# Ending each block of neighbourhood attention by itself, at four places of a head pair

## The chip, the cores and the metric

The kernel runs on one core of one Trainium2 chip. The core has a matrix engine (PE: matmuls, with PEld for its weight loads), a vector engine (DVE), a scalar engine for activation functions (ACT), a general engine (POOL), a queue engine (SP) that issues transfers, and 16 DMA engines. Each engine works through its own queue in order and waits at an instruction until what it needs is there. The metric is the time of one execution on the device in microseconds (us); it was run three times, and the median counts.

## The reference, cut to what matters

Two layers are computed on 2048 latent tokens (a grid of 32 rows by 64 columns) and 256 context tokens, of width 1024. The change is in the attention of layer 1 alone. There, each of 16 heads (64 wide) lets every token look at a window of 8 x 16 tokens around it and at all context tokens:

```python
def one_row(args):
    qr, r = args
    ...
    s_lat = jnp.einsum('bqhd,brkhd->bhqrk', qr, kb, preferred_element_type=jnp.float32) * scale
    s_lat = s_lat + bias.astype(jnp.float32)[None]
    s_lat = jnp.where(col_mask[None, None, :, None, :], s_lat, -jnp.inf).reshape(...)
    s_ctx = jnp.einsum('bqhd,bchd->bhqc', qr, k_ctx, preferred_element_type=jnp.float32) * scale
    p = jax.nn.softmax(jnp.concatenate([s_lat, s_ctx], axis=-1), axis=-1).astype(v.dtype)
    o = jnp.einsum('bhqk,bkhd->bqhd', p[..., :kr * GRID_W], vb.reshape(bsz, kr * GRID_W, h, d))
    return o + jnp.einsum('bhqc,bchd->bqhd', p[..., kr * GRID_W:], v_ctx)
...
y = jnp.dot(o.reshape(h.shape[0], h.shape[1], C_WIDTH) * jax.nn.silu(z_x), w_out)
```

## The kernel before, in words

Layer 1's attention is the function `odd_attention`. Everything stays in float32 accuracy: q and k are each split into a high and a low part.

**Pairs, tiles, blocks.** The 16 heads are taken as 8 pairs (`j` from 0 to 7), one head on the lower 64 partitions and one on the upper 64. The 2048 queries of a pair form four blocks of 512 (8 grid rows each). The keys are cut the other way: 16 latent key tiles (`n` from 0 to 15: four groups of 8 grid rows by four groups of 16 columns) and two context key tiles. A latent key tile is looked at by a rectangle of queries that reaches over two or three blocks; a context tile is looked at by all, block after block. This makes 24 score tiles a pair: 16 latent and 4 x 2 context ones, in the order `units`: context tiles of block 0, latent tile 0, context of block 1, latent tiles 1 to 3, context of block 2, latent 4 to 7, context of block 3, latent 8 to 15. Block 0 has all its parts after latent tile 7, block 1 after tile 11, blocks 2 and 3 after tile 15.

**One score tile.** PE writes the scores (`scores`, L1785: eight matmuls) into a buffer `st` of PSUM. There are only two of these (two banks each), so the scores of a tile wait until those of the tile before last have been read. For a latent tile DVE reads them: it adds the bias table (L1961) and writes to a buffer `opt` in SBUF, of which there are 11; ACT then takes the exponential in place (L108, a helper of all activations). For a context tile ACT reads the scores itself. Some tiles later the tile's tail follows: PE multiplies the exponentials with the values and accumulates into one PSUM bank `o` for each block, of which there are four (L1797 for context, L1815 for latent tiles), and POOL adds the exponentials to `oacc`, the sums for the denominators (L1821; one buffer for blocks 0 and 1, one for 2 and 3). Tails are collected in the list `pend` and put out two at a time by `flush`, whenever five are pending. The sums of two context tiles start `oacc` (L1806, on DVE for the even blocks, on POOL for the odd ones).

**Ending blocks.** `finish_blocks` ends one or two blocks: PE sums `oacc` over the partitions, times -2 (L1840, the denominators, into an `st` buffer); ACT copies them to SBUF, takes the logarithm and then the exponential of its negative, which is the reciprocal; DVE multiplies denominator and reciprocal (L1849, for a correction step), the reciprocal and the gates (L1851), corrects the accumulated output (L1854), multiplies it with the gated reciprocal (L1855); POOL issues the store to `RT1` (L1856). The function is a generator in three parts: denominators and copy; the logarithm; all the rest. `flush` starts it (list `late`: after how many flushes, which blocks), and `end` puts out one part after each score tile. Before the change, pairs 0 to 6 end blocks 0 and 1 together after tile 11's tail and blocks 2 and 3 together after tile 15's tail. Tails lag behind the scores, so both endings fall into the beginning of the next pair. The last pair ends block 0 after tile 7, block 1 after tile 11, and 2 and 3 together.

**Gates and order.** The gates of a pair (`z1`, two halves of 1024 queries) are loaded by `gates` into one buffer, `os4`, on SP's queue. All these loads are in one chain. A call `issue_after(x)` places the instructions issued under it behind the instruction `x` in the scheduler's order; otherwise the order of the code decides. So an engine's queue mixes biases, exponentials, tails and endings, and what stands ahead in a queue is done first.

After pair 7's tiles comes the output projection. During pair 7 its weights are loaded into `opt` buffers and split into high and low parts on ACT and DVE (L1299).

Of the kernel before, what the change touches and what calls it, by code (L numbers as in the profile page):

```python
# [17 lines left out]
P = 128  # L18
D = 1024
# [69 lines left out]
class Kern:  # L89
# [1630 lines left out]
    def odd_attention(self, out, pools, left, wout):  # L1720
# [4 lines left out]
        with ExitStack() as es:  # L1725
# [82 lines left out]
            def tail(n, pts, j, V, O, acc, _):  # L1808
                g, c = divmod(n, 4)
                (r0, nr), (c0, w) = rect("k", g, c)  # L1810
                done = {7: [0], 11: [1], 15: [2, 3]}.get(n, [])
# [10 lines left out]
                if n == 11:  # L1822
                    done = [1] if j == 7 else [0, 1]
                elif j < 7 and n == 7:
                    done = []
                if done:
                    late.append([2 if (j, n) == (7, 15) else 1, done, j, O, acc])
                return mm

            def gates(j, hf):  # L1830
                Z[j, hf] = self.tl(gp, [P, D], "os4", bufs=1)
                self.load(Z[j, hf][:], self.z1[j, :, hf * D : hf * D + D])

            def finish_blocks(bbs, j, O, acc):

                n, hf, o0 = len(bbs), bbs[0] // 2, bbs[0] % 2 * 512
# [11 lines left out]
                self.act(rc[:, :n], ln[:, :n], AF.Exp, scale=-1.0)  # L1848
                nc.vector.tensor_tensor(out=ln[:, :n], in0=dc[:, :n], in1=rc[:, :n], op=ALU.mult)  # L1849
                flat = rc[:, :n].rearrange("p b c -> p (b c)")  # L1850
                nc.vector.tensor_tensor(out=flat, in0=flat, in1=Z[j, hf][:, o0 : o0 + n * 512], op=ALU.mult)  # L1851
                for b, bb in enumerate(bbs):
                    o = O.pop(bb)[:].rearrange("p r c -> p (r c)")
                    nc.vector.scalar_tensor_tensor(out=o, in0=ln[:, b], scalar=2.0, in1=o, op0=ALU.add, op1=ALU.mult)  # L1854
                    nc.vector.tensor_tensor(out=rc[:, b], in0=o, in1=rc[:, b], op=ALU.mult)  # L1855
# [31 lines left out]
            Q, K, V, Z, tabs, raw = {}, {}, {}, {}, {}, {}  # L1887
# [11 lines left out]
            pend, late, ends, OA, first_sums = [], [], [], {}, {}  # L1899
# [20 lines left out]
            def end(after):  # L1920

                with self.tc.issue_after(after.ins):
                    if ends and next(ends[0], self) is self:
                        ends.pop(0)

            for j in range(8):
                OA[j] = {}, {}
                for s, (kind, n, u) in enumerate(units):
                    g, c = divmod(n, 4)
                    if s in (1, 10) and j + s > 1:  # L1930
                        gates(*((j - 1, 1) if s == 1 else (j, 0)))
# [38 lines left out]
                    end(ex)  # L1970
# [61 lines left out]
            while ends:  # L2032
                end(ex)
# [3 lines left out]
            while ends:  # L2037
                end(ex)
# [185 lines left out]
```

## Time and profile before

| what | us |
|---|---|
| median of three runs | 3561.03 |
| lowest and highest of the three | 3557.43, 3561.45 |
| the profiled execution | 3562.45 |
| its span in the profile | 3560.7 |
| PE busy in the span | 3446.4 (97%) |
| DVE, ACT, POOL busy | 2411.3, 1463.3, 1041.8 |
| mean granted clock of PE | 0.987 |

The span runs from the first instruction to the last; the execution's own time is 1.75 us longer. Layer 1's attention lies between about 2960 and 3400 us of the span. A timeline row reads: start, length, engine, line, operation, output and inputs by the program's names, shape, count, and in brackets how long the engine was idle before and what ended that. Rows of instructions that overlap or follow closely are merged. The chain of waits is followed back from the last instruction. PEq, SPq and the like are an engine's queue.

### The profile page before, as it was taken

The page shows a single profiled execution, that of the slowest core. Times are in us where ns is not written, and L with a number is a line of the kernel's source. Part 1 is how long each engine was busy: PE and PEld are TensorE (multiplying, and loading weights), DVE is VectorE, ACT ScalarE, POOL GpSimd, SP SyncE. Part 2 cuts the span into 40 slices and gives each one's busy share as a digit, 9 for nine tenths or more (in the row PEclk, how much of TensorE's full clock was granted, in tenths as well). Part 3 has the DMA queues.
Part 4 walks back from the last instruction along what each step waited for, and adds up shares of the span by engine and source line. Part 5 has one row for each costly group of instructions (what it writes and reads, how often), then busy time and mean ns, then how long its engine had stood idle before and what let it go on. Part 6 is the DMA issues. An engine that isn't in the chain of part 4 may idle for free.

```text
span 3560.7 us, 54719 instructions
## 1 busy us (share of the span) xinstructions
PE 3446.4 (97%) x20228; PEld 2671.1 (75%) x20228; DVE 2411.3 (68%) x4494; ACT 1463.3 (41%) x2570; POOL 1041.8 (29%) x1281
## 2 busy tenths in 40 slices
PE   7999998999999999999999999999999999888899
PEld 6898997888886666665557878888888886555577
DVE  4677665888885777768876654555578883555765
ACT  5454552111114554546663344454322224555532
POOL 1333431111111333322211133333111115766611
PEclk9999999999999999999999999999999999999999
DMA  7555555233315242434526764445745546454374
GB/s 255 148 155 163 146 147 157 86 98 95 105 64 162 72 132 74 124 101 145 157 82 153 149 187 150 156 129 178 226 151 171 156 121 221 160 199 176 110 186 63
DMA packets 349888, 508.40 MB, mean 143 GB/s; under 512 B 32443, under 2 KB 232843, under 8 KB 342661
## 3 DMA queue, kind: packets, MB, share of 16 engines
q1 hardware_dynamic: 297364, 386.91, 35.8%
q0 software_dynamic: 29232, 82.14, 8.7%
q10 hardware_dynamic: 23024, 35.85, 2.9%
q8 instruction: 160, 2.62, 0.3%
q14 instruction: 108, 0.88, 0.1%
HBM read 325.99 MB, written 196.60 MB: 147 GB/s over the span
## 4 chain that ended last, share of the span: by engine, by line
PE 80%; DVE 7%; DMA 5%; ACT 3%; issue 2%; POOL 2%; SPq 1%; DVEq 0%; ACTq 0%; POOLq 0%
PE gm L133 10%; PE gm L131 10%; PE gm L132 10%; PE st L1175 10%; PE av L1085 7%; PE mx L705 4%; PE st L1785 4%; PE o L1815 2%; PE o L1364 2%; PE pu L1364 2%; PE st L1364 1%; PE pj L1364 1%; PE mx L1697 1%; ACT opt L108 1%; DMA adaw<-ada_w 1%
## 5 line engine op out<-in xcount | busy, mean ns | idle before, releaser
L706 DVE TENSOR_REDUCE mm<-mx 128x1 f32<-128x512 f32 (+1 forms) x656 | 389.4, 629 | 85.1 <-PE mx L705 78.1
L108 ACT ACTIVATE apt<-st 128x1024 f32<-128x1024 f32 (+1 forms) x296 | 300.2, 1015 | 303.7 <-PE st L1175 284.4
L1182 DVE TENSOR_TENSOR acc<-acc,apt 128x1024 f32<-128x1024 f32 x256 | 340.7, 1331 | 83.2 <-ACT apt L108 64.3
L1175 PE MATMUL st<-aq,akh 64*128 64x512 f32 x1728 | 312.2, 408 | 1.3 <-ACT apt L108 1.0
L1085 PE MATMUL av<-apt,av 128*64 128x512 f32 x1152 | 265.8, 598 | 0.0
L1821 POOL TENSOR_TENSOR oacc<-oacc,opt 128x528 f32<-128x528 f32 (+4 forms) x192 | 227.6, 1207 | 73.8 <-ACT opt L108 67.6
L705 PE MATMUL mx<-mk,mq 96*128 96x512 f32 (+1 forms) x656 | 236.1, 373 | 5.3 <-DMA mq<-QC 5.3
L1175 PE MATMUL st<-aq,akl 64*128 64x512 f32 (+1 forms) x1152 | 230.7, 390 | 0.0
L1961 DVE TENSOR_TENSOR opt<-st,tab 128x496 f32<-128x496 f32 (+16 forms) x288 | 124.5, 485 | 148.4 <-PE st L1785 148.4
L108 ACT ACTIVATE u<-gm 128x352 f32<-128x352 f32 (+1 forms) x140 | 68.7, 497 | 375.7 <-PE gm L133 206.2
L1703 DVE CUSTOM_DVE_ANT_1 mx<-mx,mtab 128x105 f32<-128x105 f32 (+14 forms) x576 | 183.0, 340 | 49.3 <-PE mx L1697 35.4
L1175 PEld LDWEIGHTS st<-aq,akh 64*128 64x128 f32 x1728 | 152.9, 185 | 82.8 <-ACT apt L108 29.4
L1085 PEld LDWEIGHTS av<-apt,av 128*64 128x64 f32 x1152 | 76.3, 136 | 135.2 <-issue 133.9
L108 ACT ACTIVATE opt<-opt 128x930 f32<-128x930 f32 (+9 forms) x130 | 104.9, 807 | 147.7 <-DVE opt L1961 140.1
L1785 PE MATMUL st<-qh,kh 64*128 64x512 f32 (+6 forms) x384 | 84.2, 432 | 53.0 <-DVE opt L1961 47.2
L705 PEld LDWEIGHTS mx<-mk,mq 96*128 96x128 f32 x656 | 121.7, 189 | 17.1 <-issue 5.7
L1175 PEld LDWEIGHTS st<-aq,akl 64*128 64x128 f32 (+1 forms) x1152 | 112.3, 184 | 22.8
L1785 PEld LDWEIGHTS st<-qh,kh 64*128 64x128 f32 x384 | 38.0, 190 | 110.9 <-issue 73.4
L220 POOL TENSOR_TENSOR oss<-oss,mhalf 128x8 f32<-128x8 f32 x68 | 112.3, 1651 | 5.4
L131 PE MATMUL gm<-w1h,hhi 128*128 128x512 f32 x280 | 111.9, 400 | 0.1
L1552 DVE TENSOR_TENSOR onat<-gm,oss 128x512 f32<-128x512 f32 x68 | 46.9, 690 | 95.6 <-POOL oss L220 95.6
L131 PE MATMUL gm<-w0h,hhi 128*128 128x512 f32 x272 | 110.1, 405 | 0.0
(777 smaller groups left out, 9692.1 us busy)
## 6 DMA issues: line engine op xcount, KB each, us to landing
H<-x ACTq DMA_DIRECT2D x32, 512.0 KB
adaw<-ada_w SPq DMA_DIRECT2D x64, 256.0 KB
wraw<-w_od SPq DMA_DIRECT2D x64, 256.0 KB
K1t<-okt POOLq DMA_DIRECT2D x16, 1024.0 KB, 6.6
x<-H SPq DMA_DIRECT2D x31, 512.0 KB
mtab<-rpb_q SPq DMA_DIRECT2D x16, 899.0 KB
x<-xin SPq DMA_DIRECT2D x18, 512.0 KB
x<-xin POOLq DMA_DIRECT2D x18, 512.0 KB, 5.3
```

The source lines that it names most:

```text
L108: return self.nc.scalar.activation(out, in_, func, **kw)
L131: self.nc.tensor.matmul(out, lh(k), rh(k), start=start and j == 0, stop=False)
L132: self.nc.tensor.matmul(out, lh(k), rl(k), start=False, stop=False)
L133: yield self.nc.tensor.matmul(out, ll(k), rh(k), start=False, stop=stop and j == n - 1)
L705: mm = nc.tensor.matmul(ps[:, :w], q[:A_QK, (t % 6) * P : (t % 6) * P + P], k[:A_QK, k0 : k0 + w], start=True, stop=True)
L706: nc.vector.tensor_reduce(out=m[:, t, n : n + 1], in_=ps[:, :w], axis=AX.X, op=ALU.max)
L1085: mm = nc.tensor.matmul(O[j, nb][i * 64 : i * 64 + 64, :w], V[j, kt // TT][:, kt % TT, i * 64 : i * 64 + 64], pts[:, i, :w], start=n == 0, ...
L1175: mm = nc.tensor.matmul(ps[:, o // 64, :w], k[o : o + r, kb, kq], Q[o : o + r, qb, :w], start=m == 0, stop=m == 4)
L1182: added = nc.vector.tensor_tensor(out=acc[:, :, :w], in0=a[:, :, :w], in1=pts[:, :, :w], op=ALU.add)
L1364: self.mm = self.nc.tensor.matmul(ps, x[:, k, :], y, start=start and k == 0 and n == 0, stop=k == self.H4 - 1 and n == 2, skip_group_check ...
L1785: mm = nc.tensor.matmul(ps(i), ones[s] if k is None else k[s, ks], qs(q[s]), start=n == 0, stop=n == 3)
L1821: nc.gpsimd.tensor_tensor(out=a, in0=a, in1=pts[:, :, a0 - r0 : a1 - r0, :], op=ALU.add)
```

## The change

`tail` now hands every block to `late` by itself: block 0 after tile 7's tail and block 1 after tile 11's, in the next flush; block 2 three flushes after tile 15's tail and block 3 five flushes after it. The last pair still ends its blocks 2 and 3 together, as before. `finish_blocks` has five parts in place of three: denominators and copy; logarithm; reciprocal; the two multiplications; the rest and the store. A block 0 is put out at once, as the last pair's was before. `end` places a part behind both the tile's last bias and its exponential, where it was behind the exponential alone. The gates of the second half get a buffer of their own, `ogate` (the output projection uses it later), except in the last pair, and their load is placed two score tiles later.

```diff
                     nc.gpsimd.tensor_tensor(out=a, in0=a, in1=pts[:, :, a0 - r0 : a1 - r0, :], op=ALU.add)
-                if n == 11:
-                    done = [1] if j == 7 else [0, 1]
-                elif j < 7 and n == 7:
-                    done = []
-                if done:
-                    late.append([2 if (j, n) == (7, 15) else 1, done, j, O, acc])
+                if (j, n) == (7, 15):
+                    late.append([2, done, j, O, acc])
+                else:
+                    late.extend([{2: 3, 3: 5}.get(bb, 1), [bb], j, O, acc] for bb in done)
                 return mm
 
             def gates(j, hf):
-                Z[j, hf] = self.tl(gp, [P, D], "os4", bufs=1)
+                Z[j, hf] = self.tl(gp, [P, D], "ogate" if hf and j < 7 else "os4", bufs=1)
...
                 self.act(rc[:, :n], ln[:, :n], AF.Exp, scale=-1.0)
+                yield
                 nc.vector.tensor_tensor(out=ln[:, :n], in0=dc[:, :n], in1=rc[:, :n], op=ALU.mult)
                 flat = rc[:, :n].rearrange("p b c -> p (b c)")
                 nc.vector.tensor_tensor(out=flat, in0=flat, in1=Z[j, hf][:, o0 : o0 + n * 512], op=ALU.mult)
+                yield
                 for b, bb in enumerate(bbs):
...
-            def end(after):
-
-                with self.tc.issue_after(after.ins):
-                    if ends and next(ends[0], self) is self:
+            def end():
+
+                if not ends:
+                    return
+                with self.tc.issue_after(ex.ins), self.tc.issue_after(bias.ins):
+                    if next(ends[0], self) is self:
                         ends.pop(0)
...
-                    if s in (1, 10) and j + s > 1:
-                        gates(*((j - 1, 1) if s == 1 else (j, 0)))
+                    if s in (3, 10) and j + s > 3:
+                        gates(*((j - 1, 1) if s == 3 else (j, 0)))
...
-                    end(ex)
+                    end()
```

What this does to the queues is shown at three places. Line numbers behind the change are higher by two for the biases (L1963) and lower by one or two at the top of the ending (L1838 for the denominators, L1848 and L1850 for the first two multiplications); L1854 and L1855 are the same.

DVE at the start of a middle pair (`rl` and `opt` with 1024 or 512 elements: endings; `opt<-st,tab`: biases), before:

```order
L1849 TENSOR_TENSOR rl_28924<-opt_28907,opt_28937 128x1024
L1851 TENSOR_TENSOR opt_28937<-opt_28937,os_4956_28650 128x1024
L1854 SCALAR_TENSOR_TENSOR o_28561<-rl_28924,o_28561 128x512
L1854 SCALAR_TENSOR_TENSOR o_28598<-rl_28924,o_28598 128x512
L1961 TENSOR_TENSOR opt_28970<-st_28969,tab_28566 128x2x4x8
L1961 TENSOR_TENSOR opt_28970<-st_28969,tab_28566 128x2x4x16
L1961 TENSOR_TENSOR opt_28970<-st_28969,tab_28566 128x2x8x8
L1961 TENSOR_TENSOR opt_28970<-st_28969,tab_28566 128x2x8x16
L1806 TENSOR_TENSOR oacc_4999_28984<-opt_28927,opt_28959 128x2x512
L1855 TENSOR_TENSOR opt_28937<-o_28561,opt_28937 128x512
L1855 TENSOR_TENSOR opt_28937<-o_28598,opt_28937 128x512
L1849 TENSOR_TENSOR rl_29020<-opt_29001,opt_29037 128x1024
```

The same place now:

```order
L1848 TENSOR_TENSOR rl_28956<-opt_28939,opt_28969 128x512
L1850 TENSOR_TENSOR opt_28969<-opt_28969,os_4960_28653 128x512
L1963 TENSOR_TENSOR opt_28995<-st_28994,tab_28558 128x2x4x8
L1963 TENSOR_TENSOR opt_28995<-st_28994,tab_28558 128x2x4x16
L1963 TENSOR_TENSOR opt_28995<-st_28994,tab_28558 128x2x8x8
L1963 TENSOR_TENSOR opt_28995<-st_28994,tab_28558 128x2x8x16
L1806 TENSOR_TENSOR oacc_5010_29009<-opt_28959,opt_28982 128x2x512
L1854 SCALAR_TENSOR_TENSOR o_28590<-rl_28956,o_28590 128x512
L1855 TENSOR_TENSOR opt_28969<-o_28590,opt_28969 128x512
L1963 TENSOR_TENSOR opt_29066<-st_29065,tab_28558 128x2x124
L1963 TENSOR_TENSOR opt_29066<-st_29065,tab_28558 128x2x248
```

Only block 1's ending, at half the width, is left around latent tile 0's four biases; the biases of tile 1 follow it, where the first multiplication of blocks 2 and 3 stood.

DVE around latent tiles 9 to 11 of the same pair, before:

```order
L1961 TENSOR_TENSOR opt_29273<-st_29272,tab_28566 128x2x465
L1961 TENSOR_TENSOR opt_29285<-st_29284,tab_28566 128x2x465
L1961 TENSOR_TENSOR opt_29302<-st_29301,tab_28566 128x2x15x16
L1961 TENSOR_TENSOR opt_29302<-st_29301,tab_28566 128x2x15x7
L1961 TENSOR_TENSOR opt_29315<-st_29314,tab_28566 128x2x8x8
```

Now:

```order
L1963 TENSOR_TENSOR opt_29327<-st_29326,tab_28558 128x2x465
L1848 TENSOR_TENSOR rl_29317<-opt_29315,opt_29319 128x512
L1963 TENSOR_TENSOR opt_29339<-st_29338,tab_28558 128x2x465
L1850 TENSOR_TENSOR opt_29319<-opt_29319,os_5038_29158 128x512
L1854 SCALAR_TENSOR_TENSOR o_29058<-rl_29317,o_29058 128x512
L1855 TENSOR_TENSOR opt_29319<-o_29058,opt_29319 128x512
L1963 TENSOR_TENSOR opt_29356<-st_29355,tab_28558 128x2x15x16
L1963 TENSOR_TENSOR opt_29356<-st_29355,tab_28558 128x2x15x7
```

Block 0's ending has come between the biases of tiles 9, 10 and 11, where there were biases alone.

POOL at latent tiles 8 to 11 of the same pair (sums; the last name is the tile's exponentials), before:

```order
L1821 TENSOR_TENSOR oacc_4999_28984<-oacc_4999_28984,opt_29285 128x2x3x31
L1821 TENSOR_TENSOR oacc_5031_29172<-oacc_5031_29172,opt_29285 128x2x12x31
L1821 TENSOR_TENSOR oacc_4999_28984<-oacc_4999_28984,opt_29302 128x2x3x23
L1821 TENSOR_TENSOR oacc_5031_29172<-oacc_5031_29172,opt_29302 128x2x12x23
L1821 TENSOR_TENSOR oacc_5031_29172<-oacc_5031_29172,opt_29315 128x2x11x24
```

Now:

```order
L1821 TENSOR_TENSOR oacc_5010_29009<-oacc_5010_29009,opt_29339 128x2x3x31
L1821 TENSOR_TENSOR oacc_5045_29203<-oacc_5045_29203,opt_29339 128x2x12x31
L1856 DMA RT<-opt_29319 128x512
L1821 TENSOR_TENSOR oacc_5010_29009<-oacc_5010_29009,opt_29356 128x2x3x23
L1821 TENSOR_TENSOR oacc_5045_29203<-oacc_5045_29203,opt_29356 128x2x12x23
```

Block 0's store now stands between the sums of tile 10 and those of tile 11.

More of the change, by code (lines that the diff above doesn't have):

```diff
@@ L2032, in odd_attention @@
             while ends:
-                end(ex)
+                end()
             gates(7, 1)
@@ L2037, in odd_attention @@
             while ends:
-                end(ex)
+                end()
             PLAIN, h4 = 4, self.H4
```

## The prediction

> **What bounds the kernel now.** I read the windows from one denominator of blocks 0 and 1 to the next first, then the chain, then PE's and DVE's timelines of one pair. Chain (start, length, engine and line):
>
> ```profile
> 3005.99 1.72 PE st L1840 x8
> ...
> 3317.87 1.72 PE st L1840 x8
> ```
>
> Seven of these denominators, six periods between them: (3317.87 - 3005.99) / 6 = 51.98 us. Windows (us, PE busy, PEld, DVE, ACT, POOL, granted clock, DMA share, GB/s) of one period, of a piece inside it, and of the last pair:
>
> ```profile
> 3110.29:3161.95 51.66, 45.32 (x402) 28.47 (x400) 28.65 (x50) 26.43 (x31) 34.07 (x29) 0.97 0.47 172
> ...
> 3134.00:3136.00 2.00, 1.60 (x8) 0.96 (x9) 2.00 (x6) 0.83 (x1) 0.68 (x1) 0.73 1.01 425
> 3136.00:3138.00 2.00, 2.00 (x15) 1.48 (x16) 0.28 (x2) 1.57 (x2) 1.60 (x3) 0.50 0.98 401
> 3138.00:3140.00 2.00, 2.00 (x22) 1.46 (x18) 0.00 (x0) 0.36 (x1) 1.09 (x1) 0.91 1.11 338
> ...
> 3317.87:3384.20 66.33, 50.93 (x406) 31.02 (x404) 52.85 (x70) 37.18 (x51) 38.54 (x30) 0.90 0.37 121
> ```
>
> In a period no engine but PE is near full, and PE idles 6.3 us of it. PE's timeline shows where (in brackets the idle time before, and what ended it):
>
> ```profile
> 3110.12 1.89 PE L1840 MATMUL st<-oacc,mtwos 128*64 128x512 f32 x8
> ...
> 3113.21 0.50 PE L1785 MATMUL st<-qh,kh 64*128 64x512 f32 x2 [0.52 <-ACT opt L108]
> ...
> 3118.38 1.94 PE L1840 MATMUL st<-oacc,mtwos 128*64 128x512 f32 x8
> 3122.10 0.50 PE L1785 MATMUL st<-qh,kh 64*128 64x512 f32 x2 [1.78 <-DVE opt L1961]
> ...
> 3130.86 0.41 PE L1785 MATMUL st<-qh,kh 64*128 64x288 f32 x2 [1.29 <-DVE opt L1961]
> ...
> 3134.40 0.50 PE L1785 MATMUL st<-qh,kh 64*128 64x512 f32 x2 [2.74 <-DVE opt L1961]
> ```
>
> 0.52 + 1.78 + 1.29 + 2.74 = 6.33 us, all in the first 25 us; from there to the next denominator PE has no gap. The clock rows add a second loss: after the idle stretch the granted clock is 0.73, 0.50 and 0.91 in three windows of 2 us, 0.54 + 1.00 + 0.18 = 1.7 us. So PE's own work is 51.66 - 6.33 - 1.72 = 43.6 us. DVE's timeline over the same stretch names the cause:
>
> ```profile
> 3112.85 0.90 DVE L1961 TENSOR_TENSOR opt<-st,tab 128x272 f32<-128x272 f32 x4 [2.84 <-PE st L1785]
> 3117.35 1.23 DVE L1849 TENSOR_TENSOR rl<-opt,opt 128x1024 f32<-128x1024 f32 x1 [3.60 <-ACT opt L108]
> 3118.67 1.23 DVE L1851 TENSOR_TENSOR opt<-opt,os 128x1024 f32<-128x1024 f32 x1
> 3119.81 1.29 DVE L1854 SCALAR_TENSOR_TENSOR o<-rl,o 128x512 f32<-128x512 f32 x2
> 3121.01 0.94 DVE L1961 TENSOR_TENSOR opt<-st,tab 128x64 f32<-128x64 f32 x4
> ...
> 3127.25 2.56 DVE L1849 TENSOR_TENSOR rl<-opt,opt 128x1024 f32<-128x1024 f32 x1 [2.97 <-ACT opt L108]
> 3129.73 0.98 DVE L1961 TENSOR_TENSOR opt<-st,tab 128x248 f32<-128x248 f32 x2
> 3130.64 1.51 DVE L1851 TENSOR_TENSOR opt<-opt,os 128x1024 f32<-128x1024 f32 x1
> ```
>
> The endings of two block pairs follow each other. Bias additions (L1961), which alone free the two score buffers, stand in DVE's queue behind 1024-wide multiplications that wait for ACT: 3.60 and 2.97 us of waiting with biases queued behind it.
>
> **The change, part by part.** What one block's ending costs can be read in the last pair, which already ends blocks 0 and 1 singly (ACT, then DVE):
>
> ```profile
> 3366.70 0.58 ACT L108 ACTIVATE opt<-st 128x512 f32<-128x512 f32 x1
> 3367.30 0.63 ACT L108 ACTIVATE rl<-opt 128x512 f32<-128x512 f32 x1
> ...
> 3369.93 1.32 DVE L1849 TENSOR_TENSOR rl<-opt,opt 128x512 f32<-128x512 f32 x1
> ...
> 3372.21 1.63 DVE L1851 TENSOR_TENSOR opt<-opt,os 128x512 f32<-128x512 f32 x1
> 3373.76 0.68 DVE L1854 SCALAR_TENSOR_TENSOR o<-rl,o 128x512 f32<-128x512 f32 x1
> ...
> 3376.30 0.68 DVE L1855 TENSOR_TENSOR opt<-o,opt 128x512 f32<-128x512 f32 x1
> ...
> 3391.09 0.76 DVE L1849 TENSOR_TENSOR rl<-opt,opt 128x512 f32<-128x512 f32 x1 [1.84 <-ACT opt L108]
> ```
>
> The last row's time is the first multiplication with POOL idle, 1.32 and 1.63 are both with POOL at work. The same shows at full width: 1.23 us at 3117.35 and 2.56 at 3127.25, where POOL's timeline has
>
> ```profile
> 3102.41 13.64 POOL L1821 TENSOR_TENSOR oacc<-oacc,opt 128x144 f32<-128x144 f32 x12
> 3124.81 0.55 POOL L1856 DMA_DIRECT2D RT<-opt  x1 [8.76 <-ACT opt L108]
> 3126.35 2.38 POOL L1806 TENSOR_TENSOR oacc<-opt,opt 128x1024 f32<-128x1024 f32 x1 [0.99 <-ACT opt L108]
> 3128.80 2.27 POOL L1821 TENSOR_TENSOR oacc<-oacc,opt 128x576 f32<-128x576 f32 x1
> ```
>
> Counts for a pair: PE keeps its 16 denominator matmuls, in four groups of 0.9 us in place of two of 1.72, so its 43.6 us stay. ACT gets six instructions more, each half as long: 4 x (0.58 + 0.63 + 0.63) against 2 x 3.1 is +1.2 us, hidden in the 25 us in which ACT idles; what counts is where PE waits for a copy. DVE has the same elements. Now the waits that are left, from the start of block 1's denominator (time 0):
>
> (a) The copy of the denominator holds a score buffer. Before, the next scores waited 0.52; the denominator and copy are now 0.86 and 0.44 shorter, of which the scores of tile 15, in between, take part: 0.1, and as much after block 2's: 0.2.
>
> (b) Block 1's first multiplication ran at 3117.35, 7.06 after 3110.29. The denominator takes 0.86 less and Ln and Exp 0.4 less each: 5.4. Behind it stand the second one and tile 0's bias, 0.76 + 0.7 + 0.94 without POOL, 1.32 + 1.63 + 0.94 with it: the buffer is free at 7.8 to 9.3. PE comes to that buffer after 3118.38 - 3110.12 - 1.72 - 0.52 = 6.0 us of work, the short denominator (0.9), the wait (0.1) and one tile's scores (1.0, half of the two tiles' 1.98 in the chain below): 8.0. A wait of 0 to 1.3; 0.5, POOL being nearly through its run of sums. The waits of 1.29 and 2.74 go: nothing but biases is left in DVE's queue there.
>
> (c) Block 2's two multiplications go ahead of tile 4's bias, block 3's four operations ahead of tile 8's. PE has attention-value products and a denominator to do there (over 2 us before it needs the buffer). Bounds 0 and 0.9, and 0 and 0.6: I take 0.5 and 0.3.
>
> (d) Block 0's ending. Tile 11's bias stands behind the second multiplication and two more. Chain (scores of two tiles, of tiles 11 and 12, products of two tiles), and one bias of a wide tile from DVE's timeline:
>
> ```profile
> 3297.45 1.98 PE st L1785 x16
> ...
> 3311.93 1.33 PE st L1785 x16
> 3313.26 1.56 PE o L1815 x24
> ```
>
> ```profile
> 3091.07 1.13 DVE L1961 TENSOR_TENSOR opt<-st,tab 128x930 f32<-128x930 f32 x1 [1.44 <-PE st L1785]
> ```
>
> PE, at tile 11's scores, has 1.33 + 1.56 = 2.9 us to do until it needs the buffer that this bias frees. DVE starts tile 10's bias some 0.3 us before, an estimate (the first multiplication's 1.32 lies ahead of it, while PE has a context product to do): 1.13 + 1.63 + 0.68 + 0.68 + 0.9 (tile 11's bias, like the rows of 0.90 to 0.98) = 5.0 us. 5.0 - 0.3 - 2.9 = 1.8 us of waiting (0.9 if POOL is idle, which its 13.64 us without a gap at this place speak against).
>
> Sum: 0.2 + 0.5 + 0.5 + 0.3 + 1.8 = 3.3 us where there were 6.3, and no idle stretch of the old kind, so the 1.7 us of low clock go too: 43.6 + 3.3 = 46.9 us. Six periods: 6 x (51.98 - 46.9) = 30.5 us less. **The first pair** gains block 0's denominator and (d): 0.9 + 2.1 = 3 us more. **The last pair** takes over blocks 2 and 3 of pair 6. There DVE is busy 52.85 of 66.33 us, and it stands idle until the first product of the weight split:
>
> ```profile
> 3335.12 2.47 DVE L1299 TENSOR_TENSOR wo0l<-opt,wo0h 128x512 fp32r<-128x512 f32 x1 [3.29 <-ACT wo0h L108]
> ```
>
> That is 17.2 us after the denominator; now only block 1's ending lies ahead of it, and it can start at about 11.5. Of these 5.7 us four multiplications beside POOL's work take back 4 x 0.6: -3.5 us (0 to -6).
>
> The gate loads are costed at nothing. SP's timeline:
>
> ```profile
> 3068.34 0.33 SPq L113 DMA_DIRECT2D os<-z  x1
> 3068.76 0.38 SPq L113 DMA_DIRECT2D qh<-Q  x1
> ```
>
> The half-1 gates waited for blocks 0 and 1, and the next pair's loads behind them. With a buffer of their own they wait for nothing late, and all those loads are issued some 8 us sooner, at a DMA share of 0.47. If that cover went, block 2 would wait for its gates, about as long as the old endings did (2.7 us).
>
> Total: -30.5 + 3 - 3.5 = -31 us. The profiled execution took 3562.45 (span 3560.7), which makes 3531.5; the median of the runs shown is 3561.03, which makes 3530. **Forecast: 3531 us.** What is not shown (how often a multiplication meets POOL) bounds it: with no contention and only the copies' waits 44.5 us a period, 3513; with every contended piece on the path, below.
>
> **Rivals.** *POOL's sums hold the multiplications up longer.* The wait of 1.33 (2.56 - 1.23) could be one for a whole POOL operation, so that halving the width doesn't halve it. Then six multiplications a pair (blocks 2, 3, 0) cost 2.0 in place of 1.3 to 1.6, 3 us, of which two thirds fall on PE's waits: 49 us a period, 6 x 3 less, first pair +4, last -1.5: 3546. For it: 1.32 and 1.63 at half width are more than half of 2.56 and 1.51. Against: much of that DVE time lies behind PE work. The Trainium skill, "SBUF — State Buffer", section "Who interferes with whom", states it so: a DVE instruction with two SBUF inputs and a GpSimd one that reads SBUF take turns on one port, and the later blocks until the other is done. By that rule 3546 would be the result; the rows at 512 agree in direction, and do not settle it.
>
> *The waits only move.* Four endings in front of biases wait as long as two did, 6 us in all: 3561. Against: 1.29 and 2.74 came from two endings following each other.
>
> *Slower: POOL becomes the bound.* Block 0's store (L1856) is queued on POOL ahead of tile 11's sums, which block 1's denominator on PE needs. Before, 13.64 us of sums ran without a gap across that denominator. If POOL waits there for L1855, and four multiplications take turns with it (4 x 1.3) and two issues (0.55) come in, the sum is up to 6 us late, PE idles and the clock drops (1.7): 46.9 + 5.8 + 1.7 = 54.4 a period, 2.4 x 6 + 3: 3578. It decides once POOL is over 3.3 us late there. Against: the store should be ready by then, and POOL idled 8.76 us a period.
>
> **How the numbers follow.** Forecast (own range 3518 to 3540) 0.56; POOL's longer holds, 3546, 0.20; better still, under 3518, 0.08; waits only moved 0.08; slower 0.08. The range of 8 in 10 is 3515 to 3557. A measurement of this kernel tells about 0.2% (7 us) from no change. Faster by more: 0.56 + 0.20 + 0.08 less the upper end of the second, 0.82; within, 0.09; slower, 0.09.
>
> **What would show it.** Right: denominators (L1838) about 47 us apart; no PE wait over 2 us in a period, the longest one before tile 13's scores, ended by DVE's bias; clock 1.00 throughout. Wrong: first multiplications of 2 us and more (second case); PE's denominator waiting for POOL's sums (slower); waits of 2 us and more at tiles 4, 8 and 11 (moved).

## The result, and the profile after

| | before | after |
|---|---|---|
| median of three runs, us | 3561.03 | 3539.31 |
| lowest and highest | 3557.43, 3561.45 | 3538.20, 3539.32 |
| span of the profiled execution | 3560.7 | 3537.5 |
| PE, DVE, ACT, POOL busy | 3446.4, 2411.3, 1463.3, 1041.8 | 3442.3, 2438.7, 1465.6, 1052.0 |

The ratio after to before is 0.9941, with a 95% interval of 0.9918 to 0.9964: faster by 0.6%, 21.7 us. The forecast was 3531 (−31), its own range 3518 to 3540.

PE's timeline of the changed kernel, block 1's denominator (L1838) of the first and of the seventh pair:

```profile
3006.89 1.03 PE L1838 MATMUL st<-oacc,mtwos 128*64 128x512 f32 x4
...
3298.36 1.03 PE L1838 MATMUL st<-oacc,mtwos 128*64 128x512 f32 x4
```

(3298.36 - 3006.89) / 6 = 48.58 us a period; before it was 51.98, forecast was 46.9. So the six periods gave 20.4 us where 30.5 were expected. The two ends came out as forecast: up to the first of these denominators the attention takes 39.7 us (37.2 before: +2.5, forecast +3), and from the last one to the end of the span 239.1 (242.8 before: -3.7, forecast -3.5).

Windows of the changed kernel (columns as in the windows of before: us, PE, PEld, DVE, ACT, POOL busy, granted clock, DMA share, GB/s), for three of the periods and for three slices of 2 us in the first of them:

```profile
3055.88:3104.49 48.61, 45.49 (x405) 27.90 (x402) 32.84 (x54) 26.76 (x37) 34.87 (x30) 0.96 0.50 183
...
3202.73:3247.57 44.84, 43.90 (x406) 26.97 (x402) 29.96 (x54) 26.91 (x37) 33.59 (x29) 1.00 0.54 195
3247.57:3298.36 50.79, 46.74 (x407) 28.88 (x403) 33.94 (x54) 26.99 (x37) 36.98 (x33) 0.93 0.51 180
...
3096.00:3098.00 2.00, 0.26 (x4) 0.26 (x6) 2.00 (x3) 0.28 (x1) 0.10 (x1) 1.00 0.00 0
3098.00:3100.00 2.00, 2.00 (x24) 1.67 (x24) 1.97 (x4) 0.70 (x1) 1.15 (x2) 0.59 0.00 0
3100.00:3102.00 2.00, 2.00 (x18) 1.33 (x16) 1.27 (x6) 1.39 (x2) 1.99 (x4) 0.56 0.02 4
```

Five of the six periods take 48.5 to 50.8 us, and one takes 44.84. The same program, with the same instructions, has two lengths of a period. PE's, DVE's and POOL's timelines of the first of these periods tell what the long ones have:

```profile
3091.20 1.13 DVE L1963 TENSOR_TENSOR opt<-st,tab 128x930 f32<-128x930 f32 x1 [1.90 <-PE st L1785]
3092.25 4.40 DVE L1848 TENSOR_TENSOR rl<-opt,opt 128x512 f32<-128x512 f32 x1
3096.57 1.11 DVE L1963 TENSOR_TENSOR opt<-st,tab 128x930 f32<-128x930 f32 x1
...
3092.15 3.95 POOL L1821 TENSOR_TENSOR oacc<-oacc,opt 128x144 f32<-128x144 f32 x4
...
3097.74 0.39 PE L1785 MATMUL st<-qh,kh 64*128 64x264 f32 x2 [2.98 <-DVE opt L1963]
...
3098.44 3.02 PE L1815 MATMUL o<-opt,ov 128*64 128x72 f32 x24
```

Read it from the bottom. PE idles 2.98 us before tile 12's scores; the two slices after that have a clock of 0.59 and 0.56, which costs (1 - 0.59) x 2 + (1 - 0.56) x 2 = 1.7 us more (the tails at 3098.44 take 3.02 us in place of about 1.6 elsewhere in the period). PE waited for tile 10's bias, the third row. That bias stood in DVE's queue behind one instruction: block 0's first multiplication, 4.40 us long. It ends 0.55 us after the last of POOL's four sums (3092.25 + 4.40 = 3096.65; 3092.15 + 3.95 = 3096.10). In the short period the same instructions read:

```profile
3239.12 0.68 DVE L1848 TENSOR_TENSOR rl<-opt,opt 128x512 f32<-128x512 f32 x1
3239.72 1.12 DVE L1963 TENSOR_TENSOR opt<-st,tab 128x930 f32<-128x930 f32 x1
3240.75 1.39 DVE L1850 TENSOR_TENSOR opt<-opt,os 128x512 f32<-128x512 f32 x1
...
3239.17 7.04 POOL L1821 TENSOR_TENSOR oacc<-oacc,opt 128x144 f32<-128x144 f32 x6
```

Here the multiplication began 0.05 us ahead of the first of these sums, and took 0.68; in the long period it began 0.10 us behind. PE's only wait of that short period is 0.78 us, so its own work is 44.84 - 0.78 = 44.06 us, and the long period is 44.06 + 2.98 + 1.7 = 48.7. The fourth and the sixth period are longer still, 49.71 and 50.79: their mean clock is 0.93 in place of 0.96, and the sixth has a second wait, of 0.93.

A string of sums does not always hold a multiplication up to its end. In the short period the second multiplication (3240.75) begins inside the string and ends at 3242.14, 4 us before the string does. In the long period block 3's two multiplications fall into a row of six sums:

```profile
3084.38 1.64 DVE L1848 TENSOR_TENSOR rl<-opt,opt 128x512 f32<-128x512 f32 x1
3086.12 0.98 DVE L1850 TENSOR_TENSOR opt<-opt,ogate 128x512 f32<-128x512 f32 x1
...
3081.80 6.96 POOL L1821 TENSOR_TENSOR oacc<-oacc,opt 128x682 f32<-128x682 f32 x6 [0.91 <-ACT opt L108]
```

They end at 3086.02 and 3087.10, and the row of sums at 3088.76. The sum that the first one met, taken alone, runs from 3083.97 to 3085.47: the multiplication ended 0.55 us behind that one sum, with three more to follow it without a gap. So a multiplication can get through after one sum, as block 3's does in all six periods, or only after all of them, as block 0's does in five of six. What decides which of the two happens is not shown by any run here.

No other wait of that long period is over 0.3 us. Blocks 1, 2 and 3, ended singly, cost PE nothing there.

### The profile page after: what moved, and what is told of

Its sections match the earlier page's. It is cut to its first block, busy times and chain, and to the rows that moved or that the text cites. A ratio compares the mean times of both kernels' runs of the same rounds, so it can differ in the third digit from the quotient of the medians.

```text
span 3537.5 us, 54848 instructions
## 1 busy us (share of the span) xinstructions
PE 3442.3 (97%) x20228; PEld 2663.8 (75%) x20228; DVE 2438.7 (69%) x4522; ACT 1465.6 (41%) x2612; POOL 1052.0 (30%) x1295
## 5 line engine op out<-in xcount | busy, mean ns | idle before, releaser
L1703 DVE CUSTOM_DVE_ANT_1 mx<-mx,mtab 128x105 f32<-128x105 f32 (+14 forms) x576 | 183.1, 340 | 48.5 <-PE mx L1697 35.8
L1963 DVE TENSOR_TENSOR opt<-st,tab 128x496 f32<-128x496 f32 (+16 forms) x288 | 124.5, 484 | 107.8 <-PE st L1785 106.1
L1785 PEld LDWEIGHTS st<-qh,kh 64*128 64x128 f32 x384 | 37.7, 190 | 102.4 <-issue 48.6
L1552 DVE TENSOR_TENSOR onat<-gm,oss 128x512 f32<-128x512 f32 x68 | 46.9, 690 | 95.8 <-POOL oss L220 95.8
L133 PE MATMUL gm<-w1h,hlo 128*128 128x512 f32 x280 | 110.0, 393 | 0.0
```

What stands on the lines that cost most here:

```text
L1703: nc.vector.tensor_tensor_reduce(out=s, in0=s, in1=tb[:, ri : ri + rn, ci : ci + cn], scale=1.0, scalar=-3e38, op0=ALU.add, op1=ALU.max, a ...
L1785: mm = nc.tensor.matmul(ps(i), ones[s] if k is None else k[s, ks], qs(q[s]), start=n == 0, stop=n == 3)
L1963: bias = nc.vector.tensor_tensor(out=pt[:, :, ro : ro + rn, co : co + cn], in0=ps[:, :, ro : ro + rn, d + co : d + co + cn], in1=tabs[j][: ...
```

## The experiments

The profile suggests a theory: the single blocks make the gain, and what is missing of it is block 0's multiplication, starved (kept waiting) by POOL. The runs had to tell apart (1) what carries the gain, and (2) what block 0 costs, and why. Since the code ahead of the attention ends up to 9 us earlier or later from one profile to the next (the first scores start at 2968.8 in the profile of before, at 2959.8 in the fourth run below), mechanisms are judged by the period, and times by the ratio to runs of before on the same chip.

| run | what it is | median, us | ratio to before | period, us |
|---|---|---|---|---|
| 1 | block 0's multiplications one bias later | 3545.27 | 0.9955 (0.9938 to 0.9973) | 51.04 |
| 2 | gap in POOL's string | 3533.38 | 0.9926 (0.9910 to 0.9942) | 47.62 |
| 3 | blocks two and two, new places | 3520.93 | 0.9893 (0.9877 to 0.9909) | 46.59 |
| 4 | single blocks, three parts | 3553.56 | 0.9987 (0.9977 to 0.9996) | 51.08 |
| 5 | 0 and 1 together, 2 and 3 singly | 3528.55 | 0.9919 (0.9905 to 0.9934) | 47.42 |
| 6 | gates and bias queue alone | 3556.11 | 1.0001 (0.9991 to 1.0010) | 52.04 |
| 7 | no first multiplications for block 0 | 3511.11 | 0.9876 (0.9860 to 0.9893) | 44.87 |
| 8 | block 0's multiplications two biases later | 3542.13 | 0.9959 (0.9944 to 0.9974) | 49.49 |
| 9 | POOL does block 0's first multiplication | 3517.93 | 0.9889 (0.9875 to 0.9902) | 45.93 |
| 10 | run 3 again, beside runs 9 and 11 | 3521.63 | 0.9900 (0.9886 to 0.9914) | 46.6 |
| 11 | the changed kernel again | 3539.59 | 0.9947 (0.9932 to 0.9962) | 48.8 |

Periods are the distance between the first and the seventh denominator of block 1 (or of blocks 0 and 1), over six.

### What carries the gain: runs 3, 4 and 6

**Run 3, blocks two and two again, in the new places.** In `tail`:

```diff
-                done = {7: [0], 11: [1], 15: [2, 3]}.get(n, [])
+                done = [] if j < 7 and n == 7 else [0, 1] if j < 7 and n == 11 else stops
...
-                    late.extend([{2: 3, 3: 5}.get(bb, 1), [bb], j, O, acc] for bb in done)
+                    late.append([1, done, j, O, acc])
```

> The changed kernel with the blocks ended two and two again (0 and 1 after tile 11, 2 and 3 after tile 15), while the five parts, their places behind biases and exponentials, and the gates' own buffer stay. Theory (the single blocks make the gain, by taking the 1024-wide operations and one ending behind the other out of DVE's queue): nearly all of the gain is gone, 3553 to 3562 us, with PE's waits of 1 to 3 us at two or three places of a period. Rival (queuing the parts behind biases makes it): 3535 to 3545 us.

Measured: 3520.93 us. The theory that the single blocks carry the gain fell with this run; the rival was right in kind, and even it expected too little: undoing them made the changed kernel faster. Its window over the six periods, PE's waits in the second one and DVE's timeline there:

```profile
3001.91:3281.48 279.57, 263.86 (x2405) 165.20 (x2402) 164.64 (x300) 158.04 (x180) 207.80 (x169) 1.00 0.52 191
...
3051.60 0.49 PE L1785 MATMUL st<-qh,kh 64*128 64x512 f32 x2 [0.53 <-ACT opt L108]
...
3059.28 0.50 PE L1785 MATMUL st<-qh,kh 64*128 64x512 f32 x2 [0.58 <-DVE opt L1964]
3060.88 0.50 PE L1785 MATMUL st<-qh,kh 64*128 64x512 f32 x2 [0.40 <-ACT opt L108]
3071.79 0.50 PE L1785 MATMUL st<-qh,kh 64*128 64x512 f32 x2 [1.03 <-DVE opt L1964]
...
3055.74 1.23 DVE L1849 TENSOR_TENSOR rl<-opt,opt 128x1024 f32<-128x1024 f32 x1 [3.60 <-ACT opt L108]
...
3058.19 0.94 DVE L1964 TENSOR_TENSOR opt<-st,tab 128x64 f32<-128x64 f32 x4
...
3060.19 1.28 DVE L1855 SCALAR_TENSOR_TENSOR o<-rl,o 128x512 f32<-128x512 f32 x2
3061.38 1.28 DVE L1856 TENSOR_TENSOR opt<-o,opt 128x512 f32<-128x512 f32 x2
3065.01 1.00 DVE L1964 TENSOR_TENSOR opt<-st,tab 128x248 f32<-128x248 f32 x2 [2.35 <-PE st L1785]
3065.92 1.32 DVE L1849 TENSOR_TENSOR rl<-opt,opt 128x1024 f32<-128x1024 f32 x1
```

Four waits, 0.53 + 0.58 + 0.40 + 1.03 = 2.54 us, none long, and a clock of 1.00 over six periods. The rows tell how. Before, the second ending's first multiplication stood ahead of a tile's bias and waited 2.97 us for ACT's exponential with that bias behind it; here it stands behind that bias (3065.92), and when its turn comes ACT is done: no wait. And the corrections of the attention values (L1855) stand behind tile 0's bias (3058.19), not ahead of it. These are the parts' new places, not the blocks' size: the multiplications are 1024 wide as before. POOL has a string of four sums beside the second ending too (3066.22 to 3074.15), but the first multiplication begins 0.3 us ahead of it, and the second one (3068.07) gets through inside it in 1.54 us.

**Run 4, single blocks with an ending in three parts.**

```diff
                 self.act(rc[:, :n], ln[:, :n], AF.Exp, scale=-1.0)
-                yield
...
                 nc.vector.tensor_tensor(out=flat, in0=flat, in1=Z[j, hf][:, o0 : o0 + n * 512], op=ALU.mult)
-                yield
```

> The changed kernel with an ending in three parts again (the two new breaks taken out), single blocks kept: for blocks 1, 2 and 3 all four multiplications are put out together. Theory (breaks matter little, since a short ending has slack): PE waits up to 0.9 us more in a period before tiles 0 to 4, 3539 to 3545 us. Rival (the breaks carry half of the gain): 3550 us and more.

Measured: 3553.56 us, the rival's side: nearly the whole gain gone. PE's waits in the second period:

```profile
3059.86 0.50 PE L1785 MATMUL st<-qh,kh 64*128 64x512 f32 x2 [1.09 <-DVE opt L1961]
...
3075.56 0.49 PE L1785 MATMUL st<-qh,kh 64*128 64x480 f32 x2 [1.22 <-DVE opt L1961]
...
3094.97 0.59 PE L1785 MATMUL st<-qh,kh 64*128 64x264 f32 x2 [2.89 <-DVE opt L1961]
```

Block 0's wait is as in the changed kernel (2.89), and waits of 1.1 to 1.2 us are there at two more endings, where the four DVE operations of a block now stand together in front of a bias. Since a half clock follows the 2.89 too, 44.06 + 5.2 + 1.7 = 51.0, the measured 51.08.

**Run 6, gates' buffer, their later load and the bias queue, without single blocks and without the two new breaks.** The edits of runs 3 and 4 together.

> Blocks two and two again and an ending in three parts again; of the change only the gates' own buffer, their later load and the queuing behind a bias as well as an exponential are left. On DVE, ACT and POOL the instructions then stand as in the kernel before. Theory (the gates are worth nothing; queuing behind a bias moves nothing as long as the four kinds of multiplications come in one part): 3556 to 3562 us, period 52.0. Rival (the gates' earlier loads let the next pair's loads and so its first tiles start sooner): 3545 us or less.

Measured: 3556.11 us, ratio 1.0001, period 52.04, PE's waits those of before (third period: 0.52, 1.78, 1.29, 2.74). As the theory said: the gates are worth nothing, although SP issues the next pair's first load 2.4 us after the denominator of blocks 0 and 1 in this run, 10.2 us after it in the kernel before; and the bias queue alone moves nothing. The reverse, five parts behind exponentials alone with blocks in pairs, was not run; in that program the instructions of DVE, ACT and POOL stand in the same order as in run 6. So the breaks alone move nothing either: it takes both, the breaks and the place behind the bias.

The four corners give the periods 51.98 (pairs, old places: before), 46.59 (pairs, new places), 51.08 (singles, three parts) and 48.58 (singles, new places: the change). **The places carry the gain: 5.4 us a period. The single blocks give 0.9 in the old places and take 2.0 in the new ones.**

### What block 0 costs: runs 1, 2, 7 and 8

**Run 1: block 0's multiplications one bias later**, so that little but their own place changes (the store comes later, too). In `flush`, for pairs 0 to 6:

```diff
                     if x[1] == [0]:
-                        for _ in ends.pop():
-                            pass
+                        next(ends[-1])
```

(the other parts then follow in `end`, as for the other blocks).

> The changed kernel with block 0's two multiplications one bias later: in DVE's queue they stand behind tile 10's bias instead of ahead of it; the store moves behind tile 11's sums. Theory (block 0's first multiplication gets no turn while POOL's string of sums runs, 4.4 us, and what costs is that tile 10's bias is queued behind it): the multiplication may still take 2 to 4 us, but tile 10's bias is out; PE's wait of 2.98 us before tile 12's scores goes, at most 1 us is left before tile 13's, no half clock; the period falls from 48.6 to 45 to 46 us and the time to about 3522 us. Rival (four operations of an ending ahead of a bias cost PE 3 us wherever they stand): the wait moves to tile 13's scores and stays 2 to 3 us; 3536 to 3542 us.

Measured: 3545.27 us; PE's longest wait moved by a tile, as the rival said, and grew to 3.67 us. DVE, POOL and PE in the third period:

```profile
3092.95 4.85 DVE L1848 TENSOR_TENSOR rl<-opt,opt 128x512 f32<-128x512 f32 x1 [0.54 <-ACT opt L108]
...
3091.19 6.06 POOL L1821 TENSOR_TENSOR oacc<-oacc,opt 128x144 f32<-128x144 f32 x6
...
3099.53 0.43 PE L1785 MATMUL st<-qh,kh 64*128 64x352 f32 x2 [3.67 <-DVE opt L1966]
```

The theory's first half stands (4.85 us, ending 0.55 after POOL's string, 3097.80 against 3097.25); its second half does not: the string had by then grown by tile 10's sums to six, so it held the next bias just as long.

**Run 2: a gap in the string.** One-element copies on POOL behind the sums of tiles 8 and 9 (the scheduler put two of them between tile 8's sums and tile 9's):

```diff
                     nc.gpsimd.tensor_tensor(out=a, in0=a, in1=pts[:, :, a0 - r0 : a1 - r0, :], op=ALU.add)
+                    if n in (8, 9) and j < 7:
+                        nc.gpsimd.tensor_copy(out=gap[:1, :1], in_=a[:1, 0, :1, 0])
```

> The changed kernel with tiny copies (one element, POOL) put behind the sums of tiles 8 and 9, so that POOL's string of sums is broken once behind tile 8's two pieces. Theory A (DVE gets its turn at the first gap between POOL operations that are not issued back to back): block 0's first multiplication takes about 2.4 us instead of 4.4, PE's wait falls from 3.0 to about 1 us, the period to 46 or 47: 3527 to 3532 us. Theory B (DVE comes through only where POOL's queue is empty): it still takes 4.4 us or a little more; 3539 to 3543 us. Theory C (a turn after every single POOL operation, and the 4.4 us have another cause): no change either, 3539 us, and the multiplication would not end at the end of POOL's string.

Measured: 3533.38 us. DVE and POOL (the lines are two further down: L1850 is the first multiplication, L1852 the second, L1856 and L1857 the last two operations):

```profile
3085.97 2.35 DVE L1850 TENSOR_TENSOR rl<-opt,opt 128x512 f32<-128x512 f32 x1
...
3089.28 1.95 DVE L1852 TENSOR_TENSOR opt<-opt,os 128x512 f32<-128x512 f32 x1
3091.16 0.68 DVE L1856 SCALAR_TENSOR_TENSOR o<-rl,o 128x512 f32<-128x512 f32 x1
3091.87 0.69 DVE L1857 TENSOR_TENSOR opt<-o,opt 128x512 f32<-128x512 f32 x1
...
3085.89 1.87 POOL L1821 TENSOR_TENSOR oacc<-oacc,opt 128x144 f32<-128x144 f32 x2
3087.72 0.88 POOL L1823 COPY pad<-oacc 1x1 f32<-1x1 f32 x2
3088.56 2.12 POOL L1821 TENSOR_TENSOR oacc<-oacc,opt 128x186 f32<-128x186 f32 x2
...
3091.23 2.11 POOL L1821 TENSOR_TENSOR oacc<-oacc,opt 128x186 f32<-128x186 f32 x2
```

The time that theory A gave came out: the multiplication took 2.35 us in place of 4.40, ending 0.56 us after the two sums (3088.32 against 3087.76). The reason that it gave did not: the copies follow the sums without idle time on POOL (3087.72), so that it was no gap that let the multiplication in. Why the copies do it is not shown. PE's wait before tile 12 fell from 2.98 to 0.93. The second multiplication met the next two sums (1.95), and 1.83 us came up before tile 13's scores (where the prediction's step (d) put a wait of 1.8), so part of the gain was given back: 47.62 where 46 or 47 was expected; in two of the six periods a stretch of half clock follows that wait. The rows at 3091.16 and 3091.87 show who is not held up: operations with one input in PSUM take 0.68 and 0.69 beside POOL's sums.

**Run 7: block 0 without its first two multiplications** (the reciprocal's correction and the gate are left out for that block in pairs 0 to 6):

```diff
+                if j == 7 or bbs != [0]:
                     nc.vector.tensor_tensor(out=ln[:, :n], in0=dc[:, :n], in1=rc[:, :n], op=ALU.mult)
                     nc.vector.tensor_tensor(out=flat, in0=flat, in1=Z[j, hf][:, o0 : o0 + n * 512], op=ALU.mult)
```

> The changed kernel without block 0's first two multiplications in pairs 0 to 6 (the correction of the reciprocal and the gate are left out for that block; its attention values are then wrong), so that block 0 has no DVE operation with two inputs from SBUF. Theory (these two, starved by POOL's string, are the whole price of the single block 0): no PE wait over 1 us, clock 1.00, period 44.5 to 45.2 us, 3515 to 3520 us. Rival (the price is block 0's denominator, copy and bias order themselves): the wait before tile 12 or 13 stays 2 us and more, 3532 to 3539 us.

Measured: 3511.11 us and a period of 44.87, the theory's in the period and 4 us below its range in time. The window over the six periods:

```profile
2999.98:3269.19 269.21, 264.60 (x2406) 161.45 (x2403) 171.38 (x312) 161.72 (x217) 209.58 (x181) 1.00 0.55 199
```

PE 264.60 of 269.21 us, at a clock of 1.00. The two multiplications are 14 instructions of DVE, 0.7 us each when alone, some 10 us in all; what goes with them is (0.9947 - 0.9876) x 3560 = 25 us (run 11's ratio less this one's).

**Run 8: two biases later**, with all of block 0's parts in `end` (the same place in `flush`, with no `next`).

> The changed kernel with block 0's ending queued in parts behind the biases like the other blocks' (not put out at once): its first multiplication stands among tile 11's and 12's biases, two biases later than in the changed kernel. Theory (it costs only where a string of POOL sums runs): POOL idles 2.8 us about there; the multiplication takes 0.7 to 1.6 us if it falls into that gap, PE's wait is under 1 us and the time 3515 to 3522 us; if it starts after the next string has begun it takes 2 to 4 us again and the time stays 3535 to 3545 us. Rival (late endings make block 1's denominator or the store late): den of block 1 waits for POOL, over 3550 us.

Measured: 3542.13 us, the case "after the next string has begun": there was no next string, the first had grown to eight sums.

```profile
3090.37 4.65 DVE L1848 TENSOR_TENSOR rl<-opt,opt 128x512 f32<-128x512 f32 x1
...
3086.78 7.69 POOL L1821 TENSOR_TENSOR oacc<-oacc,opt 128x144 f32<-128x144 f32 x8
```

3095.02 against 3094.47: once more 0.55 us behind the string. So it is in five of the six periods; in the third the multiplication got through after 3.05 us (3140.84), with sums still following, and PE's wait was 2.08 there in place of 3.7. Block 1's denominator did not wait for POOL.

### Better versions: runs 5, 9, 10 and 11

**Run 5: blocks 0 and 1 together after tile 11, 2 and 3 singly**, to have the cheap half of each.

```diff
+                elif done == [0, 1]:
+                    late.append([1, done, j, O, acc])
```

> The changed kernel with blocks 0 and 1 ended together after tile 11, blocks 2 and 3 singly as they are. Theory (of the four single endings only block 0's costs anything, because its multiplications fall on POOL's string of sums; blocks 2 and 3 singly have no PE wait, blocks 0 and 1 together cost PE 0.53 and 0.58 us): period 44.1 + 1.1 = 45.2 us, six of them 20 us less than the changed kernel's: 3510 to 3518 us, faster than both kernels. Rival (the endings disturb each other wherever they stand, so that a wait comes back behind the 1024-wide multiplications): 3521 us as with all blocks in pairs, or more.

Measured: 3528.55 us, period 47.42; the rival held. PE and DVE in the second period:

```profile
3057.45 0.50 PE L1785 MATMUL st<-qh,kh 64*128 64x512 f32 x2 [1.36 <-DVE opt L1966]
...
3055.22 1.23 DVE L1853 TENSOR_TENSOR opt<-opt,os 128x1024 f32<-128x1024 f32 x1
3056.36 0.94 DVE L1966 TENSOR_TENSOR opt<-st,tab 128x64 f32<-128x64 f32 x4
```

In run 3 the denominators of blocks 2 and 3 (1.94 us of PE) stood right ahead of the scores that waited 0.58. With those moved back, PE comes to the same buffer earlier, at 3056.09, while DVE is still in the 1024-wide multiplication, with the bias behind it: 1.36. A wait's price cannot be carried from one order into another.

**Run 9: block 0 without an operation that POOL's sums can hold up**, nothing left out. POOL itself does the first multiplication, between its sums, and the gate goes into the attention values in PSUM:

```diff
+                if j < 7 and bbs == [0]:
+                    nc.gpsimd.tensor_tensor(out=ln[:, 0], in0=dc[:, 0], in1=rc[:, 0], op=ALU.mult)
+                    o = O[0][:].rearrange("p r c -> p (r c)")
+                    nc.vector.tensor_tensor(out=o, in0=o, in1=Z[j, 0][:, :512], op=ALU.mult)
```

> The changed kernel with block 0's two starved multiplications (pairs 0 to 6) done another way, nothing left out: the first one by POOL itself, which puts it between its sums of tiles 8 and 9, and the gate multiplied into the attention values where they lie in PSUM, so that DVE has no operation with two inputs from SBUF there. Theory (the starved multiplications are all that the single block 0 costs): period 44.5 to 45.3 us as in the run without them, no PE wait over 1 us, 3512 to 3520 us, ahead of the run with all blocks in pairs by about 6 x 1.7 us. Rival (the 1.2 us more on POOL make block 0's store and tile 11's sums late): block 1's denominator waits for POOL 1 us or more, 3525 us and above.

Measured: 3517.93 us, within the theory's range; the period, 45.93, is 0.6 above it. POOL and DVE in the third period, and PE's waits:

```profile
3082.22 1.27 POOL L1850 TENSOR_TENSOR rl<-opt,opt 128x512 f32<-128x512 f32 x1
...
3077.44 0.69 DVE L1852 TENSOR_TENSOR o<-o,os 128x512 f32<-128x512 f32 x1
3079.42 2.16 DVE L1968 TENSOR_TENSOR opt<-st,tab 128x930 f32<-128x930 f32 x2 [1.29 <-PE st L1785]
...
3086.02 0.43 PE L1785 MATMUL st<-qh,kh 64*128 64x352 f32 x2 [0.99 <-DVE opt L1968]
...
3097.92 0.50 PE L1785 MATMUL st<-qh,kh 64*128 64x512 f32 x2 [0.69 <-DVE opt L1968]
```

The biases of tiles 9 and 10 now follow each other without a gap, and two waits of 0.99 and 0.69 are left. The theory had it some 10 us ahead of the blocks in pairs; run 10 below, with the blocks in pairs, came out 3.7 us behind it.

**Runs 10 and 11** are run 3 and the changed kernel again, on the chip of run 9 and in five rounds.

> The kernel with blocks two and two in the five new parts once more, beside the next one on the same chip. Theory: again 1.1% less than before, 3518 to 3525 us, and 0.5% less than the changed kernel in the same runs. Rival (that gap came from comparing runs on different chips): within 0.2% of the changed kernel.

> The changed kernel itself, for the comparison on one chip. Theory: 0.6% less than before, 3533 to 3542 us, five or six periods of 48.5 us with a PE wait of 3.0 us before tile 12's scores, none or one of 45. Rival: a time near that of the blocks in pairs.

Measured: 3521.63 and 3539.59 us, ratios 0.9900 and 0.9947: the theory both times. Run 11's profile has five periods with a wait of 2.93 to 3.03 us and one with 0.77. Runs 9 and 10 both beat the changed kernel, by 0.6 and 0.5% of medians; between the two (0.9889 and 0.9900) the intervals overlap.

## Why the prediction was right, and where not

The time lies 0.7 us inside the upper end of the forecast's own range, with 21.7 us of gain where 31 were forecast.

**What bounds the kernel: right.** DVE operations of an ending in front of biases, 6.33 us of PE's waits and 1.7 of low clock: take them away (run 3: waits 2.54, clock 1.00) and the period falls by 5.4.

**PE's own work, 43.6 us: 0.5 too low.** 44.06 in the short period.

**Steps (a), (b) and (c), 0.2 + 0.5 + 0.8: too high.** In the long period shown, no wait over 0.3 is left at these places, near the lower end, 0, of the bounds for (b) and (c). Only the sixth period has one of 0.93, within (b)'s bounds.

**Step (d), block 0: the step that failed.** The prediction put 1.8 us before tile 13's scores, from tile 11's bias behind the second multiplication and the last two operations, with 1.32 us for the first. The first one took 4.40 in five of six periods; tile 10's bias is behind it, so the wait is one tile sooner, before tile 12, and 2.98 long. The 1.32 was the duration of one meeting with POOL, and POOL's timeline of the kernel before, which the prediction did not lay beside it, shows which:

```profile
3368.39 2.32 POOL L1821 TENSOR_TENSOR oacc<-oacc,opt 128x144 f32<-128x144 f32 x2
3371.17 2.12 POOL L1821 TENSOR_TENSOR oacc<-oacc,opt 128x186 f32<-128x186 f32 x2 [0.47 <-ACT opt L108]
```

That multiplication (3369.93, 1.32) came in the last 0.8 us of a string that ended at 3370.71, and ended 0.54 us behind it. That its length is set by what POOL has still to do, and not by the multiplication, could have been read there; that four sums would hold it could not. The half clock was to go with the old waits; it came back with this one, 1.7 us. Measured: 44.06 + 2.98 + 1.7 = 48.7, forecast 43.6 + 3.3 = 46.9. The miss of 1.8 is (d)'s 1.2 too little, the clock's 1.7 and the base's 0.5, less the 1.5 that (a) to (c) had too much. Run 7 shows the whole of it: without the two multiplications 44.87.

**First pair, last pair, gates: right.** First pair +2.5 (+3), with one wait of 1.57 (3003.80). Last pair -3.7 (-3.5): the first product of the weight split starts at 3309.31, 10.95 us after the denominator, where 11.5 was forecast and 17.2 was before. Gates: a ratio of 1.0001 for run 6.

**What makes the gain: wrong in the reason.** The prediction priced single blocks at their new places in one sum, and put the end of the waits of 1.29 and 2.74 down to the endings no longer following each other. In run 3 the endings follow each other as before, and one wait of 1.03 is left in their place: the new places of the parts do the work, and the split into single blocks loses 2 us a period on top of them and gives only 0.9 by itself (run 4). That the time came out inside the range is in part luck: the 1.5 us too much in (a) to (c) stand against the 2.9 too little in (d) and the clock.

**The rivals.** *POOL's sums hold the multiplications up longer*, 3546: the right mechanism with another shape, one instruction of 4.4 us in place of six of 2.0, and the time fell between it and the forecast. The Trainium skill, "SBUF — State Buffer", section "Who interferes with whom", calls the port pair that DVE shares with GpSimd an exclusive lock, and says that the order of issue decides who blocks. The rows agree on who meets whom (0.68 us beside POOL with one input in PSUM, 4.40 with two in SBUF) and on the order of issue (0.05 us ahead: 0.68; 0.10 behind: 4.40). On how long, the rows differ among themselves: block 3's multiplication waited for one sum of POOL, block 0's for four. *Waits only move*: no. *POOL becomes the bound*: no; block 1's denominator waited for POOL in none of the periods, and block 2's 0.29 us.

**What it said would show it.** Denominators 47 us apart: 48.6. No wait over 2 us: one of 2.98. A clock of 1.00: 0.93 to 0.97, and 1.00 in the one short period. First multiplications of 2 us and more: yes, block 0's alone (blocks 1 to 3: 0.7 to 1.8).

## What to carry to other kernels

When two edits go in together, price each without the other: here, where an operation stands in its queue was worth 5.4 us a period, and how it is cut was worth less than nothing as long as block 0's multiplications met POOL's sums (in run 9, which avoids that, single blocks are 0.7 us a period ahead of pairs). Before an operation with both inputs in SBUF is moved on DVE, look at what POOL's timeline has at the new place; if it is a run of operations without a gap, count one operation of it as the least and the whole run as the most that the wait can be, with whatever is queued behind. A wait that has been priced in one order of the work has to be priced again in the next one, since what covers it has moved too.

## What the runs showed of the hardware that was not expected

Block 0's first multiplication, with both inputs in SBUF, began behind the first of a string of POOL additions and ended 0.55 us after the last: 2.35 us with two sums (run 2), 4.40 with four, 4.85 with six and 4.65 with eight (it started later in the last two). That is no rule for every meeting: in the same profiles block 3's multiplications ended 0.55 us after a single sum, in the middle of a string, and what decides it stays open. Two one-element copies between the sums were enough to let block 0's through. Periods of 44.84 and of 48.5 us and more stand in one and the same execution, and what differs between them at first is which of two instructions began first, by 0.1 us.

And after 3 us without a matmul PE ran at a clock of 0.59 and 0.56 for the next 4 us. In run 3, with waits of up to 1.06 us, it stayed at 1.00. In between it went both ways: behind waits of 1.36 us (run 5) and of 1.83 us (run 2) the clock fell in two of the six periods each (to 0.67 and 0.50 in the slices of 2 us from 3105.50 of run 5), and stayed at 1.00 in the others.
